# Neighbourhood attention in a two-layer encoder: the two heads of a pair taken together, with the products' order across the halves of the TensorE array changed

## The chip, the cores and the metric

One core of one Trainium2 chip runs the whole program. The metric is device time in microseconds (us) of one execution; three executions of the kernel before gave a median of 902.64 us (899.07 to 903.24).

## The reference, cut to what matters

The program is a two-layer encoder trunk on 256 tokens of 1024 features, in float32. Layer 0 computes from one normed input `h` two things side by side, a state-space scan and a neighbourhood attention with 16 heads of 64 features; both go through one output projection, and a channel mixer follows. Layer 1 is an mLSTM with its own channel mixer. What is changed lies in the attention alone:

```python
q, k, v = jnp.split(qkv.astype(jnp.float32), 3, axis=-1)     # on a grid of 4 rows x 64 columns
...
s = jnp.einsum('bwhd,biwjhd->bhwij', q_r, k_win) + bias.transpose(0, 2, 1, 3)[None]
p = jax.nn.softmax(s.reshape(Bsz, NA_HEADS, GRID_W, kh * NA_KW), axis=-1).reshape(s.shape)
return jnp.einsum('bhwij,biwjhd->bwhd', p, v_win)
```

Each query sees all 4 rows and a window of 16 columns.

## The kernel before

**The weight stream.** Every weight matrix comes in slabs of 128x2048 (1 MB each). A slab is loaded by SyncE (L169) into one of three `raw` buffers. Each of its halves is split into two exact parts, `wh` by ScalarE (L193) and `wl` by VectorE (L194), and three products stand for one exact one: high by high, high by low, low by high (L215 to L217 where weights are the stationary operand, L226 where tokens are). `run` (L145) goes through the list of slabs, and after each half `adv` (L97) advances two queues of side work, `qa` (the scan) and `qb` (the attention), by as many steps as `PLAN0` (L40) gives for that half. A step is what stands between two `yield`s. The instructions are then ordered once, at build time, by a scheduler with a cost model: on each engine an instruction of the earliest place in the program that is ready by the model goes first. On the chip each engine runs this order.

**The attention.** The q and k projections (`na_qk_unit`, L827) leave for each pair of heads a tile `qk`, in which head `i` of the pair holds partitions `64*i` to `64*i+63`. After each k half, `na_side` (L845) of one pair is put on `qb`; there are 8 pairs. A tile of 128 queries is half of the columns of all grid rows (index `f`), and sees 40 columns of each of the 4 rows, 160 keys. In order of its steps, `na_side` does for each head of a pair: two score products (L853, 64 partitions to 128 columns of the stationary operand, 160 moving columns each) into one PSUM bank, the load of the bias table (L857, SyncE), and two fused add-and-minimum operations (L862, VectorE); then two exponentials (L869, ScalarE), the reciprocal (L871) and two scalings (L873, ScalarE) into a padded tile `np`; then four transposes (L878) and a copy to `nap` (L881, ScalarE). After both heads come four value products (L888, 128 partitions to 64 columns, 256 moving columns): both key halves `kk` of head 0, then both of head 1. Head `i` fills output partitions `64*i` to `64*i+63` of one bank, and one copy (L894) takes it to `nay`. These are 7 steps a pair. A float32 product stands in the trace as two weight loads and two matmuls, so there are 4 records of L853 for a head, and 8 of L888 for a pair.

```python
for f in range(2):
    nc.tensor.matmul(out=ps[:, f * 160:(f + 1) * 160], lhsT=qk[rows, 0, f * P:(f + 1) * P], ...)
...
for i in range(2):
    for kk in range(NT):
        nc.tensor.matmul(out=ps[i * 64:(i + 1) * 64, :256], ...)
```

**Banks and buffers.** `bank()` (L79) gives PSUM banks by turns from two pools of two, `sd` and `yp`; scan and attention share them. The projections use four other banks (`acc`). The tiles `rpb` (bias), `nas`, `namx`, `nap` have two buffers each. The scan's products with 48 partitions (L800, L805) build a 128x512 bank that ScalarE takes the exponential of (L808).

Of the kernel before, what the change touches and what calls it, by code (L numbers as in the profile page):

```python
# [10 lines left out]
F32 = mybir.dt.float32  # L11
# [3 lines left out]
ALU = mybir.AluOpType  # L15
# [3 lines left out]
P = 128  # L19
D = 1024  # L20
KT = D // P
NT = 2
# [3 lines left out]
LOW = 1.0e-17  # L26
# [11 lines left out]
SUB_LEAD = 250  # L38
# a slab, steps of the side work (scan, attention) after each half of it, slabs of the modulation after it
PLAN0 = (("v0", 0, 8, 1), ("v1", 0, 5, 0), ("v2", 0, 6, 0), ("q0", 1, 8, 0), ("k0", 4, 3, 0), ("v3", 4, 5, 0),  # L40
# [11 lines left out]
class Trunk:  # L52
# [24 lines left out]

# [1 line left out]
    def bank(self):  # L79
# [32 lines left out]

# [1 line left out]
    # A slab is one transfer; it is split into its two exact parts in `nh` pieces of `hw` columns.  # L114
    def slab(self, ap, nh=2, hw=1024, bufs=None, ada=None, tag=None):
# [93 lines left out]

# [1 line left out]
    def mm_ws(self, out, wh, wl, xh, xl, nk=KT):  # L211
# [16 lines left out]

# [1 line left out]
    def setup(self):  # L230
# [74 lines left out]

    # rows over the partitions, in two exact parts, times a column of ones on both: a broadcast
    def row_parts(self, hi_lo, rows, src):
# [3 lines left out]

# [1 line left out]
    def add_ada(self, layer, j, where):  # L313
# [56 lines left out]

# [1 line left out]
    def squares(self, views):  # L372
# [14 lines left out]

    # the end of a sub-layer for one tile of tokens, and the start of the next
    def sub_end(self, t, banks, out=None):
# [46 lines left out]

    # log(1 + e) for 0 <= e <= 1
    def log1p(self, e, shape):
# [14 lines left out]

# [1 line left out]
    def start(self):  # L455
        nc, io = self.nc, self.io
# [3 lines left out]
        def begin():  # L460
# [16 lines left out]
            self.cbk = [self.abank() for _ in range(4)] + [self.yp.tile([P, 512], F32, name="yp") for _ in range(2)]  # L477
            # zeros, and often enough to have the tensor engine at its full clock when the data arrives
            for i in range(WARM):
# [9 lines left out]

        # the columns of shift and scale for `nb` blocks of features, in slabs of K-tiles  # L490
        def block(kt0, nb, on_pe):
# [61 lines left out]

        # the half that holds B and C goes first
        convs = ([], [])
# [78 lines left out]

    # 32 columns of a projection, to tokens on the rows
    def small_unit(self, name, side):
# [15 lines left out]

# [1 line left out]
    def conv_side(self, pair):  # L654
# [31 lines left out]
    def dt_side(self, ps):  # L686
        nc = self.nc
# [8 lines left out]
        nc.vector.scalar_tensor_tensor(out=self.dt, in0=v, scalar=0.0, in1=l, op0=ALU.max, op1=ALU.add)  # L696
        # where dt is below LOW, ln(dt) = v: what lies below ln(LOW) is added to ln(max(dt, LOW))
        low = self.tmp.tile([P, NT, 32], F32, name="l1p_z", bufs=1)
# [4 lines left out]
        yield  # L703
        # running sums of dt*a inside each chunk: cs (dir, chunk, head), and what is left to its end
        ps = self.bank()
# [13 lines left out]
        self.wst = (dec[:, 4, :], dec[:, 5, :])  # L719
        # ln(dt), with a Newton step, less the running sums  # L720
        v = self.tmp.tile([P, NT, 32], F32, name="dtv", bufs=1)
# [27 lines left out]
    def ssd_side(self):  # L749
# [12 lines left out]
        yield  # L762
        # states carried from one chunk to the other, and their part of y
        for g in range(2):
# [8 lines left out]
            for d in range(2):  # L773
# [14 lines left out]
                yield  # L788
        # inside the chunks, two heads at a time: M[s, t] = (C_t.B_s) * sum over directions of decay * dt_s
        for hp in range(8):  # L790
# [33 lines left out]

# [1 line left out]
    # A tile of queries is half of the columns of all grid rows; it sees 40 columns of each row.  # L826
    def na_qk_unit(self, j, which):  # L827
# [15 lines left out]
        return fn  # L843

    def na_side(self, pair, qk):  # L845
        nc = self.nc
        pts = []
        for i in range(2):
            head = 2 * pair + i
            rows = slice(i * 64, (i + 1) * 64)  # L850
            ps = self.bank()
            for f in range(2):
                nc.tensor.matmul(out=ps[:, f * 160:(f + 1) * 160], lhsT=qk[rows, 0, f * P:(f + 1) * P],  # L853
                                 rhs=qk[rows, 1, :].rearrange("p (r w) -> p r w", w=64)[:, :, f * 24:f * 24 + 40],
                                 start=True, stop=True)
            bias = self.tmp.tile([P, 320], F32, name="rpb")
            nc.sync.dma_start(out=bias, in_=self.io["rpb"][head])  # L857
            s = self.tmp.tile([P, 320], F32, name="nas")
            mx = self.tmp.tile([P, 2], F32, name="namx")
            for f in range(2):  # L860
                fs = slice(f * 160, (f + 1) * 160)
                nc.vector.tensor_tensor_reduce(out=s[:, fs], in0=ps[:, fs], in1=bias[:, fs], op0=ALU.add,  # L862
                                               op1=ALU.min, scale=-1.0, scalar=3.0e38, accum_out=mx[:, f:f + 1])
            yield
            pad = self.npad[i]
            nsum = self.tmp.tile([P, 2], F32, name="nasum")
            win = [pad[:, f].rearrange("p (r w) -> p r w", w=64)[:, :, f * 24:f * 24 + 40] for f in range(2)]
            for f in range(2):
                nc.scalar.activation(out=win[f], in_=s[:, f * 160:(f + 1) * 160].rearrange("p (r w) -> p r w", w=40),  # L869
                                     func=AF.Exp, scale=-1.0, bias=mx[:, f:f + 1], accum_out=nsum[:, f:f + 1])  # L870
            nc.vector.reciprocal(out=nsum, in_=nsum)  # L871
            for f in range(2):
                nc.scalar.activation(out=win[f], in_=win[f], func=AF.Copy, scale=nsum[:, f:f + 1])  # L873
            yield
            ps = self.bank()
            for kk in range(NT):
                for f in range(2):
                    nc.tensor.transpose(out=ps[:, (kk * 2 + f) * P:(kk * 2 + f + 1) * P],  # L878
                                        in_=pad[:, f, kk * P:(kk + 1) * P], identity=self.ident)
            pt = self.tmp.tile([P, 512], F32, name="nap")  # L880
            nc.scalar.copy(out=pt, in_=ps)  # L881
            pts.append(pt)
            yield
        ps = self.bank()
        for i in range(2):
            head = 2 * pair + i
            for kk in range(NT):
                nc.tensor.matmul(out=ps[i * 64:(i + 1) * 64, :256], lhsT=self.v[:, kk, head * 64:(head + 1) * 64],  # L888
                                 rhs=pts[i][:, kk * 256:(kk + 1) * 256], start=(kk == 0), stop=(kk == 1))
# [7 lines left out]

# [1 line left out]
    def rows_mm(self, ps, t, i, wh, wl):  # L899
# [15 lines left out]

    # first columns after a boundary: one tile of tokens after the other
    def rows_head(self, aps, bufs, evac, late):
        nc = self.nc

        def fn(parts):  # L920
            pss = []
            for t in range(NT):
                ps = self.abank()
                ts = slice(t * P, (t + 1) * P)
                # of each half of the features first what needs only their first parts
                for q in range(2):
# [63 lines left out]

    # pairs of feature tiles in two parts, made one ahead of their use
    def pairs_of(self, n, make):
# [97 lines left out]

# [1 line left out]
    def mlp(self, layer, ada_js, head_bufs, out=None):  # L1092
# [49 lines left out]

# [1 line left out]
    def gates_side(self, ps):  # L1144
# [50 lines left out]
        yield  # L1195
        # the floor of the denominator, with tokens on the rows
        self.thr = self.big.tile([P, 2, NT, 8], F32, name="dec")
# [10 lines left out]

    # columns of the score tile of a direction: (dir, key tile) -> (first column, first query, queries)
    SPAN = {(0, 0): (0, 0, 256), (0, 1): (256, 128, 128), (1, 0): (0, 0, 128), (1, 1): (128, 0, 256)}  # L1210
# [31 lines left out]
    def ml_head(self, h, eh, el):  # L1242
# [34 lines left out]
        nc.gpsimd.tensor_tensor(out=ss, in0=ss, in1=self.nhalf, op=ALU.pow)  # L1277
        # half of the norm here, the other half of sigmoid = (1 + tanh) / 2 where the gate arrives
        for t in range(NT):
# [4 lines left out]

    # scores of two heads run ahead of the values
    def ml_side(self):
# [106 lines left out]

# [1 line left out]
def _ws(w):  # L1395
# [105 lines left out]
```

## Time and profile before

| what | value |
|---|---|
| median of three runs | 902.64 us (899.07 to 903.24) |
| profiled execution, first to last instruction (span) | 901.6 us |
| TensorE (PE) busy | 875.1 us, 97% |
| VectorE (DVE) busy | 676.5 us, 75% |
| ScalarE (ACT) busy | 499.0 us, 55% |
| mean granted TensorE clock | 0.994 |
| attention's first score product to its last value product | 99.0 to 242.7 us |

Of the profiled execution only the span is told; it lies 1.04 us below the median of the runs. PE is the matmul, PEld the weight load of the same engine, which overlaps it. Times in rows are microseconds unless marked ns. A busy PE is not PE at its peak: the end of a matmul is modelled, so how densely matmuls follow each other is read from their starts, or from the length of a piece of the chain.

### The profile page before, as it was taken

What the parts mean: (1) busy time and instruction counts of PE and PEld (TensorE: products, weight loads), DVE (VectorE), ACT (ScalarE), POOL (GpSimd) and SP (SyncE); (2) the same over time, 40 slices, a digit from 0 to 9 for tenths busy, and PEclk for the clock granted to TensorE, in tenths of its full rate; (3) what the DMA queues carried; (4) which work ended last, traced back from release to release, by engine and by line L of the source; (5) the groups of instructions that cost most, each with busy time, mean ns of one, the idle gap of its engine ahead of it and who ended that gap; (6) DMA issues with size and microseconds to landing.
All of it is one profiled execution on the core that took longest, in us unless ns stands there. A gap on an engine that the chain in (4) does not pass through costs nothing.

```text
span 901.6 us, 13452 instructions
## 1 busy us (share of the span) xinstructions
PE 875.1 (97%) x5176; PEld 750.6 (83%) x5176; DVE 676.5 (75%) x1098; ACT 499.0 (55%) x870; POOL 45.2 (5%) x68
## 2 busy tenths in 40 slices
PE   7999999999999999999998999999999899999997
PEld 6998887777787898989986998888877699999895
DVE  5869898766688777877777957996978865665754
ACT  3466885656756445445454465777556454444452
POOL 3000000000001000000001000211100100000000
PEclk8999999999999999999999999999999999999999
DMA  9866456524574567777762665645487365665651
GB/s 338 327 223 252 152 189 216 203 96 156 218 276 164 190 237 282 291 281 256 276 265 95 235 233 188 214 186 178 148 293 265 120 235 189 234 233 188 227 187 47
DMA packets 32773, 193.44 MB, mean 215 GB/s; under 512 B 4923, under 2 KB 6971, under 8 KB 11333
## 3 DMA queue, kind: packets, MB, share of 16 engines
q1 hardware_dynamic: 31536, 188.35, 57.4%
q10 hardware_dynamic: 1172, 4.24, 1.3%
q8 instruction: 40, 0.66, 0.3%
q14 instruction: 25, 0.20, 0.1%
HBM read 191.52 MB, written 1.05 MB: 214 GB/s over the span
## 4 chain that ended last, share of the span: by engine, by line
PE 79%; DVE 9%; DMA 6%; ACT 3%; issue 1%; POOL 1%; SPq 0%; POOLq 0%; DVEq 0%; ACTq 0%
PE acc L226 32%; PE acc L215 4%; PE acc L217 3%; PE acc L216 3%; PE yp L217 3%; PE sd L217 3%; PE yp L216 3%; PE yp L215 3%; PE sd L216 3%; PE sd L215 3%; DVE wl L194 3%; PE acc L930 2%; DMA raw<-in_ml_w_out 2%; DMA raw<-in_mlp_w 2%; ACT wh L193 1%
## 5 line engine op out<-in xcount | busy, mean ns | idle before, releaser
L194 DVE TENSOR_TENSOR wl<-raw,wh 128x1024 fp32r<-128x1024 f32 (+1 forms) x234 | 278.5, 1195 | 124.5 <-ACT wh L193 123.8
L193 ACT CAST wh<-raw 128x1024 fp32r<-128x1024 f32 (+1 forms) x234 | 239.2, 1027 | 217.0 <-PE acc L226 81.5
L226 PE MATMUL acc<-wh,uh 128*128 128x512 f32 x352 | 112.5, 392 | 0.3 <-ACT uh L433 0.3
L226 PE MATMUL acc<-wh,ul 128*128 128x512 f32 x352 | 111.9, 391 | 0.9 <-DVE ul L434 0.9
L226 PE MATMUL acc<-wl,uh 128*128 128x512 f32 x352 | 112.3, 391 | 0.2 <-DVE wl L194 0.2
L330 DVE SCALAR_TENSOR_TENSOR ada<-raw,cond,ada 128x1024 f32<-128x1024 f32 x80 | 102.3, 1278 | 3.7 <-DMA raw<-in_ada_w 2.1
L215 PE MATMUL acc<-hh,wh 128*128 128x256 f32 x272 | 79.0, 291 | 1.1 <-ACT xt L1349 0.9
L226 PEld LDWEIGHTS acc<-wh,ul 128*128 128x128 f32 x352 | 65.9, 188 | 15.1 <-DVE ul L434 1.3
L226 PEld LDWEIGHTS acc<-wl,uh 128*128 128x128 f32 x352 | 65.9, 188 | 14.9 <-DVE wl L194 0.6
L216 PE MATMUL acc<-hl,wh 128*128 128x256 f32 x272 | 77.8, 286 | 0.0
L217 PE MATMUL acc<-hh,wl 128*128 128x256 f32 x272 | 77.6, 289 | 0.0
L226 PEld LDWEIGHTS acc<-wh,uh 128*128 128x128 f32 x352 | 63.8, 188 | 12.2 <-ACT uh L433 0.5
L226 PE MATMUL acc<-wh,hh 128*128 128x512 f32 x176 | 70.0, 399 | 0.0
L226 PE MATMUL acc<-wh,hl 128*128 128x512 f32 x176 | 69.6, 396 | 0.0
L226 PE MATMUL acc<-wl,hh 128*128 128x512 f32 x176 | 69.5, 395 | 0.0
L217 PE MATMUL yp<-hh,wl 128*128 128x256 f32 x224 | 63.4, 283 | 0.0
L216 PE MATMUL yp<-hl,wh 128*128 128x256 f32 x224 | 63.4, 283 | 0.0
L217 PE MATMUL sd<-hh,wl 128*128 128x256 f32 x224 | 63.3, 283 | 0.0
L215 PE MATMUL yp<-hh,wh 128*128 128x256 f32 x224 | 63.3, 283 | 0.0
L216 PE MATMUL sd<-hl,wh 128*128 128x256 f32 x224 | 63.3, 283 | 0.0
L215 PE MATMUL sd<-hh,wh 128*128 128x256 f32 x224 | 63.3, 282 | 0.0
L215 PEld LDWEIGHTS acc<-hh,wh 128*128 128x128 f32 x272 | 51.9, 191 | 4.7 <-ACT xt L1349 1.6
(436 smaller groups left out, 1769.2 us busy)
## 6 DMA issues: line engine op xcount, KB each, us to landing
raw<-in_mlp_w SPq DMA_DIRECT2D x60, 1024.0 KB, 4.9
raw<-in_ada_w SPq DMA_DIRECT2D x40, 1024.0 KB, 6.5
raw<-in_ab_w_out SPq DMA_DIRECT2D x8, 1024.0 KB
raw<-in_ml_w_v SPq DMA_DIRECT2D x8, 1024.0 KB, 4.8
raw<-in_ml_w_o SPq DMA_DIRECT2D x8, 1024.0 KB, 4.8
raw<-in_ml_w_out SPq DMA_DIRECT2D x8, 1024.0 KB, 7.5
raw<-in_ada_two SPq DMA_DIRECT2D x4, 1024.0 KB
raw<-in_w_v SPq DMA_DIRECT2D x4, 1024.0 KB
```

What stands on the lines that cost most here:

```text
L193: nc.scalar.copy(out=wh[:, cs], in_=src[:, cs])
L194: nc.vector.tensor_tensor(out=wl[:, cs], in0=src[:, cs], in1=wh[:, cs].bitcast(F32), op=ALU.subtract)
L215: mm(out=out, lhsT=a, rhs=xh[:, k, :], start=(k == 0), stop=False)
L216: mm(out=out, lhsT=a, rhs=xl[:, k, :], start=False, stop=False)
L217: mm(out=out, lhsT=b, rhs=xh[:, k, :], start=False, stop=(k == nk - 1))
L226: mm(out=outs[j], lhsT=x, rhs=w[:, n0 + j * 512:n0 + (j + 1) * 512], start=first and i == 0, stop=last and i == 2)
L330: nc.vector.scalar_tensor_tensor(out=acc, in0=raw[:, q * D:(q + 1) * D], scalar=col, in1=acc, op0=ALU.mult, op1=ALU.add)
L930: nc.tensor.matmul(out=ps, lhsT=x[:, kt, ts], rhs=parts[kt // 2][wi][:, (kt % 2) * 512:(kt % 2 + 1) * 512], start=(kt == 0 and x is self.h ...
```

## The change

`na_side` takes both heads of a pair in each step. The four score products come first, each head into its own bank, in the order head 1, head 0, head 1, head 0, and each is tied behind the one before it on TensorE's queue. All four add-and-minimum operations follow. The bias tables are loaded one pair ahead, by a new function. The softmax of head 1 comes before the transposes of head 0. The value products alternate between head 1 and head 0, which is between the halves of the output's partitions. A pair still has 7 steps and takes 5 banks. The other hunks of the diff take out comments.

```diff
+    def na_bias(self, pair):
+        if pair < 8:
+            self.bias[pair] = [self.tmp.tile([P, 320], F32, name="rpb") for _ in range(2)]
+            for i in range(2):
+                self.nc.sync.dma_start(out=self.bias[pair][i], in_=self.io["rpb"][2 * pair + i])
     def na_side(self, pair, qk):
         nc = self.nc
-        pts = []
+        if pair == 0:
+            self.bias = {}
+            self.na_bias(0)
+        sps = [self.bank() for _ in range(2)]
+        with ExitStack() as order:
+            for f in range(2):
+                for i in (1, 0):
+                    rows = slice(i * 64, (i + 1) * 64)
+                    keys = qk[rows, 1, :].rearrange("p (r w) -> p r w", w=64)[:, :, f * 24:f * 24 + 40]
+                    last = nc.tensor.matmul(out=sps[i][:, f * 160:(f + 1) * 160],
+                                            lhsT=qk[rows, 0, f * P:(f + 1) * P], rhs=keys, start=True, stop=True)
+                    order.enter_context(self.tc.issue_after(last.ins))
+        bias = self.bias.pop(pair)
+        ss, mxs = [], []
         for i in range(2):
-            head = 2 * pair + i
-            rows = slice(i * 64, (i + 1) * 64)
-            ps = self.bank()
-            for f in range(2):
-                nc.tensor.matmul(out=ps[:, f * 160:(f + 1) * 160], lhsT=qk[rows, 0, f * P:(f + 1) * P],
-                                 rhs=qk[rows, 1, :].rearrange("p (r w) -> p r w", w=64)[:, :, f * 24:f * 24 + 40],
-                                 start=True, stop=True)
-            bias = self.tmp.tile([P, 320], F32, name="rpb")
-            nc.sync.dma_start(out=bias, in_=self.io["rpb"][head])
             s = self.tmp.tile([P, 320], F32, name="nas")
             mx = self.tmp.tile([P, 2], F32, name="namx")
             for f in range(2):
                 fs = slice(f * 160, (f + 1) * 160)
-                nc.vector.tensor_tensor_reduce(out=s[:, fs], in0=ps[:, fs], in1=bias[:, fs], op0=ALU.add,
+                nc.vector.tensor_tensor_reduce(out=s[:, fs], in0=sps[i][:, fs], in1=bias[i][:, fs], op0=ALU.add,
                                                op1=ALU.min, scale=-1.0, scalar=3.0e38, accum_out=mx[:, f:f + 1])
-            yield
-            pad = self.npad[i]
+            ss.append(s)
+            mxs.append(mx)
+        self.na_bias(pair + 1)
+        yield
+        for i in range(2):
+            s, mx, pad = ss[i], mxs[i], self.npad[i]
...
             nc.vector.reciprocal(out=nsum, in_=nsum)
+            yield
             for f in range(2):
                 nc.scalar.activation(out=win[f], in_=win[f], func=AF.Copy, scale=nsum[:, f:f + 1])
-            yield
+        yield
+        pts = []
+        for i in range(2):
             ps = self.bank()
...
         ps = self.bank()
-        for i in range(2):
-            head = 2 * pair + i
-            for kk in range(NT):
+        for kk in range(NT):
+            for i in (1, 0):
+                head = 2 * pair + i
                 nc.tensor.matmul(out=ps[i * 64:(i + 1) * 64, :256], lhsT=self.v[:, kk, head * 64:(head + 1) * 64],
                                  rhs=pts[i][:, kk * 256:(kk + 1) * 256], start=(kk == 0), stop=(kk == 1))
```

## Rows read from the trace of the kernel before

**Rows 1.** The page: busy time, share of the span and instructions of two engines.
```profile
PE 875.1 (97%) x5176; PEld 750.6 (83%) x5176; DVE 676.5 (75%) x1098; ACT 499.0 (55%) x870; POOL 45.2 (5%) x68
```

**Rows 2.** Busy time in stretches of the attention; columns in the first line.
```profile
core 0: us, PE busy (x) PEld busy (x) DVE busy (x) ACT busy (x) POOL busy (x), PEclk, DMA share, GB/s
98.00:125.00 27.00, 27.00 (x185) 23.19 (x185) 23.49 (x52) 21.45 (x53) 0.00 (x0) 1.00 0.49 174
125.00:155.00 30.00, 30.00 (x163) 21.94 (x161) 25.77 (x41) 22.23 (x51) 0.95 (x1) 1.00 0.55 189
...
215.00:245.00 30.00, 30.00 (x152) 21.05 (x152) 19.08 (x40) 22.13 (x58) 1.12 (x2) 1.00 0.53 192
sum 147.00, PE 147.00 PEld 112.26 DVE 109.24 ACT 100.83 POOL 3.02; mean PE 29.40 PEld 22.45 DVE 21.85 ACT 20.17 POOL 0.60
```

**Rows 3.** The chain, 98 to 245 us: shares by line, pieces (start, us, what).
```profile
by line: PE acc L226 24.9%; PE acc L216 9.1%; PE acc L215 9.1%; PE acc L217 9.0%; PE yp L888 5.5%; PE sd L888 5.4%; PE sd L853 3.9%; PE yp L853 3.8%; PE sd L878 3.2%; PE yp L800 2.6%; PE yp L878 2.6%; PE sd L819 2.5%; PE sd L783 2.5%; PE yp
...
103.97 0.74 PE sd L853 x4
112.89 0.58 PE sd L888 x2
113.83 1.01 PE sd L888 x6
121.00 0.47 PE yp L853 x2
...
131.96 1.01 PE sd L888 x4
132.97 1.36 PE acc L226 x5
...
162.44 1.16 PE acc L226 x5
167.75 1.75 PE yp L888 x8
169.50 0.74 PE yp L853 x4
```

**Rows 4.** The timeline, 173.2 to 174.6 us: start, us, engine, instruction.
```profile
173.27 0.38 PE L800 MATMUL sd<-csr,pickr 48*128 48x256 f32 x1
173.28 0.18 PEld L853 LDWEIGHTS yp<-qk 64*128 64x128 f32 x1
173.29 0.40 PE L853 MATMUL yp<-qk 64*128 64x160 f32 x1
...
173.53 0.30 PE L853 MATMUL yp<-qk 64*128 64x160 f32 x1
...
173.66 0.30 PE L853 MATMUL yp<-qk 64*128 64x160 f32 x1
...
173.80 0.30 PE L853 MATMUL yp<-qk 64*128 64x160 f32 x1
```

**Rows 5.** Who waited for whom, 98 to 245 us: total, times, longest.
```profile
PEld sd L888 <- ACT nap L881: 1.1, 2, 0.8
...
PEld sd L878 <- ACT np L873: 0.7, 2, 0.4
...
PEld yp L853 <- DVE namx L862: 0.4, 1, 0.4
```

**Rows 6.** Groups of instructions on ACT, 98 to 245 us: busy, mean ns, idle.
```profile
L193 ACT CAST wh<-raw 128x1024 fp32r<-128x1024 f32 x26 | 26.9, 1047 | 9.2 <-PE acc L216 6.5 <-PE acc L226 2.4
...
L881 ACT COPY nap<-sd 128x512 f32<-128x512 f32 x9 | 5.3, 586 | 3.9 <-PE sd L878 3.9
```

**Rows 7.** SyncE's queue, 98 to 245 us: who waited for whom.
```profile
SPq L857 <- DVE namx L862: 41.7, 11, 6.5
```

More of the change, by code (lines that the diff above doesn't have):

```diff
@@ L878, in na_side @@
                     nc.tensor.transpose(out=ps[:, (kk * 2 + f) * P:(kk * 2 + f + 1) * P],
-                                        in_=pad[:, f, kk * P:(kk + 1) * P], identity=self.ident)
+                                        in_=self.npad[i][:, f, kk * P:(kk + 1) * P], identity=self.ident)
             pt = self.tmp.tile([P, 512], F32, name="nap")
```

## The prediction

> **What bounds the kernel now.** I read the busy times first, to see which engine could hold the end: TensorE is busy for 97% of the span, VectorE for 75%, ScalarE for about half [rows 1]. A share of the whole says nothing of one stage, so I then read the stretch that holds the attention, 98 to 245 us: TensorE is busy in all of its 147 us, VectorE in 109, ScalarE in 101, the granted clock is 1.00 (the upper level, 2.4 GHz) and the DMA engines are about half busy [rows 2]. VectorE is nearest to a bound of its own between 98 and 155 us, with 49.3 of 57 us, 86%. The chain of waits comes third: from 98 to 245 us nearly every piece is TensorE's, and the attention's small products stand on it with their whole length [rows 3]. So time taken out of these products is taken out of the end, as long as nobody else becomes late, and the stages behind simply start earlier.
>
> **What the small products cost.** By the shares of the chain the scores (L853) take 3.9 + 3.8 = 7.7% of 147 us, 11.3 us; the values (L888) 5.5 + 5.4 = 10.9%, 16.0 us [rows 3]. The chain lists the scores in 16 pieces and the values in 19. A full score piece of one head, 4 records, is 0.74 us and a piece of 2 records 0.47, so a further record costs about 0.135 us and some 0.20 us of a piece is paid for coming in, however short it is. For values, 4 records are 1.01 us and 2 records 0.58: 0.215 us a record, 0.15 for coming in. Going back to full-array products also costs: five L226 records right behind a value piece are 1.36 us, five behind other work 1.16, so 0.20 us for each return [rows 3]. Six of the 35 pieces stand directly behind another one, and one behind a scan product that also uses only part of the rows; some 28 returns are left.
>
> **The change, part by part.**
>
> *Scores, both heads in one run.* The two heads use opposite halves of the array's rows and write different banks. The question is whether their matmuls then run side by side. The trace of before has one place where this happened by chance: at 173.27 us a scan product on 48 rows and a score product of head 1 start 0.02 us apart, and the four score records keep their own pace (173.29, 173.53, 173.66, 173.80) although scan products run between them [rows 4]. So I take it that head 0's four records hide wholly under head 1's, and a pair's scores cost one piece of 0.74 us: 8 x 0.74 = 5.9 instead of 11.3. **Gain 5.4 us.** Bounds: with no overlap a pair costs 0.74 + 4 x 0.135 = 1.28, in all 10.2, a gain of 1.1; no row suggests more than 5.4.
>
> *Values, alternating.* They overlap by columns, and this too is in the trace: a piece of six records takes 1.01 us, just as one of four does, so two of the six cost nothing [rows 3]. In that piece products of both heads stood side by side, because head 0's first product had gone ahead at 112.89. With head 1, head 0, head 1, head 0 every record has a partner, so 8 records take the time of 4: 8 x 1.01 = 8.1 instead of 16.0. **Gain 7.9 us.** There is a second reason in it: before, head 0's values could start before head 1's transposes were done, which tore them into pieces of two; now the first product needs head 1's probabilities, the last to be ready, and all four follow. Without overlap a pair costs the 1.75 us of the piece of eight [rows 3], in all 14.0, a gain of 2.0.
>
> *Fewer returns.* 16 runs instead of 35 pieces; with one or two of them joined about 15 returns instead of 28: 13 x 0.20. **Gain 2.6 us.** Together 5.4 + 7.9 + 2.6 = 15.9 us.
>
> *Here a rule of the skill speaks against me.* The trace lets a record of the second head pass one of the first, or six records could not fit into four records' time. The Trainium skill ("TensorE: Matmul & The Clock Gate", Part 3) says that matmuls are a strict FIFO in start and end, with no reordering. As one product is two records on the same half, by that rule only every second record would find a partner at once; the piece of six speaks against it. It is a rival below.
>
> *What comes in the way.* The two score banks are taken at once, one of each pool, and both are held until four add-and-minimum operations in a row are done; the scan then has two banks instead of three for a moment. Waits of TensorE on such work are in the trace, but small: 1.1 us in two cases for the copy to `nap`, 0.7 for the scaled probabilities, 0.4 for the reductions [rows 5]. Since the order of the instructions was made by a model before the run, and TensorE now gets through a pair's products about 2 us sooner, it will arrive early more often. The price has no row of its own. At best the 2.2 us of these waits go (a gain); at worst all values of a pair stand behind a cast of 1.05 us and the copy of 0.59 us on ScalarE [rows 6], 1.63 us a pair, 13.1 us in all. I take 0.4 us a pair, nearest to the waits that the trace has: **loss 3.2 us.**
>
> *What costs nothing.* The bias tables: 16 loads as before, on SyncE's queue, now behind both heads' reductions of the pair before. Their waits of before (41.7 us in 11 cases, the longest 6.5) reached no other engine [rows 7], because three slabs of weights are buffered; with 26 casts of half a slab in 147 us [rows 6] a slab lasts some 11 us. If that cover were gone, a wait of 6.5 us would reach TensorE through a late slab. The split of the softmax into other steps moves ScalarE and VectorE work by a step and adds none; it is hidden under projections, with ScalarE at 101 of 147 us. What is late next is VectorE between 98 and 155 us: if a third of the saving falls there, 49.3 us of work stand in 52, so the saving fits but with little room.
>
> **The sum.** 15.9 - 3.2 = 12.7 us off the profiled span of 901.6 gives 888.9; the median of the runs lies 1.04 us above that span, so 889.9, rounded to **890 us**.
>
> **The rivals.**
>
> 1. *FIFO.* If a head's second record can't be passed, a score run costs one slot of 0.135 us more and a value run one of 0.215: 8 x 0.35 = 2.8 us, 892.8 us. For it: only one clean case of passing. Against: that case. This is what the rule named above would give. Chance 0.10.
>
> 2. *Torn runs.* Scan or projection products that become ready in the model may be put between the four products. Before, one head's scores were torn, at 121.00 [rows 3]. A tear of a score run costs 0.20 + 0.20 us, of a value run 0.15 + 0.20; if every run is torn once, 8 x 0.75 = 6.0 us, 896 us. For it: many values were torn before. Against: the scores are now tied behind each other, and the four values wait for the same last copy. Chance 0.12.
>
> 3. *No overlap at all:* the change doesn't do what it says. Gain 1.1 + 2.0 + 2.6 = 5.7, less the waits of 3.2: 900.1 us. Against it stand both rows of overlap; for it, that these were chance meetings, one of them with a scan product of another type. Chance 0.06.
>
> 4. *A dear wait.* The upper bound of the waits, 1.63 us a pair, leaves 2.8 us of the gain: 899.8 us. Chance 0.06.
>
> 5. *Slower: the values wait for the copy of head 1.* Before, head 0's values could fill the time in which ScalarE copies head 1's probabilities to `nap`; now nothing of the values can. If ScalarE has two casts in front of that copy, it comes 2 x 1.05 + 0.59 = 2.68 us late [rows 6], for each of 8 pairs instead of 0.4: 18.2 us, 908 us. It decides from about 2.0 us a pair on (no gain at all), 2.5 for slower by 0.5%. Against it: the copy itself waited for TensorE before, 3.9 us of idle time on ScalarE in one of its two groups [rows 6], not the other way round, and the projections can be put in between. Chance 0.06.
>
> **How the numbers follow.** The forecast (everything overlaps, small waits) has the chance 0.60 that is left. A measurement of this kernel can tell some 0.5% from no change, 4.5 us: faster means below 898.1. That holds for the forecast, the FIFO and the torn runs: 0.60 + 0.10 + 0.12 = 0.82. No overlap and the dear wait are within 0.5%: 0.12. Slower is 0.06. The range goes from all gains with the old waits gone (902.6 - 15.9 - 2.2 = 884.5) up to no overlap, 900.2; outside are the slower case and what I have missed on both sides.
>
> **What would show it.** In the profile after, the chain should list 8 score pieces of about 0.74 us with 8 records and 8 value pieces of about 1.01 with 8; the timeline should show starts of `sd` and `yp` records of the new score line within 0.02 us of each other. Pieces of 1.28 and 1.75 would mean no overlap; 0.9 and 1.2 the FIFO; pieces of 2 or 4 records torn runs. For the waits: the row of TensorE's weight load of the values waiting for `nap` would grow from 1.1 us to some 3 (forecast) or 20 (slower). The prediction is wrong if the stretch from the first score to the last value shrinks by less than 8 us, or if it shrinks as said and the end doesn't, which would mean that a later stage was held by something other than TensorE.

## The result, and the profile after

Changed kernel: **890.32 us**, the median of 4 runs (889.11 to 893.19), beside 900.86 us for the kernel before in the same comparison. The ratio is **0.9902 [0.9878, 0.9925]**, which is 8.8 us off (6.8 to 11.0). The forecast was 890.0, a gain of 12.7 us. The time fell almost on it, the gain did not, so the agreement in time is largely luck: the forecast counted from the first three runs of the kernel before (902.64), which were high; in the comparisons below, with 11 to 23 runs each, its median is 897.9 to 898.8. The two medians above differ by 10.5 us; what is told as the gain here and below is that of the ratio, which comes with an interval.

The page, busy time of the engines, which answers to [rows 1]:

```profile
PE 863.6 (97%) x5176; PEld 745.4 (84%) x5176; DVE 676.5 (76%) x1098; ACT 498.5 (56%) x870; POOL 45.9 (5%) x68
```

The number of records is the same on every engine. TensorE is busy 11.5 us less. The same stretches as in [rows 2], columns as there:

```profile
98.00:125.00 27.00, 24.18 (x174) 20.30 (x173) 22.45 (x45) 20.00 (x49) 0.00 (x0) 1.00 0.48 168
125.00:155.00 30.00, 28.80 (x159) 20.96 (x158) 26.03 (x48) 22.08 (x54) 0.95 (x1) 1.00 0.52 187
...
sum 147.00, PE 142.20 PEld 111.92 DVE 114.24 ACT 103.79 POOL 3.02; mean PE 28.44 PEld 22.38 DVE 22.85 ACT 20.76 POOL 0.60
```

Here is the first thing to see. Before, TensorE was busy in every one of these 147 us; now it sits idle for 4.8 of them, and 4.0 of those lie between 98 and 155 us. VectorE and ScalarE each do more of their work inside the stretch (+5.0 and +3.0 us), because the work behind it has moved up. The granted clock is 1.00 in both, so the clock explains nothing in this stretch.

The products themselves, from the timeline of TensorE (start, us, engine, instruction), the first pair's scores:

```profile
98.45 0.40 PE L864 MATMUL yp<-qk 64*128 64x160 f32 x1
98.45 0.40 PE L864 MATMUL sd<-qk 64*128 64x160 f32 x1
98.69 0.30 PE L864 MATMUL yp<-qk 64*128 64x160 f32 x1
98.69 0.30 PE L864 MATMUL sd<-qk 64*128 64x160 f32 x1
...
112.95 0.39 PE L217 MATMUL acc<-hh,wl 128*128 128x256 f32 x1 [1.24 <-DVE wl L194]
...
122.59 0.50 PE L226 MATMUL acc<-wh,hh 128*128 128x512 f32 x1 [1.31 <-ACT wh L193]
...
143.86 0.39 PE L215 MATMUL acc<-hh,wh 128*128 128x256 f32 x1 [1.20 <-ACT wh L193]
...
167.15 1.08 PE L907 MATMUL yp<-nap,v 128*64 128x256 f32 x8
```

Both heads' records start together, and a pair's four starts take the time that one head took. Seven of the eight score runs are whole, 8 records each; so are seven of the eight value runs (the first pair's is torn into 4 and 4). The three lines with a bracket are new waits: none is the attention's, all three are products of a projection that wait for a part of their weights (`wl` from VectorE, `wh` from ScalarE).

The chain of waits, 98 to 245 us, answers to [rows 3] (start, us, what):

```profile
113.57 1.15 DVE wl L194
114.77 6.70 DMA raw<-in_w_z
121.49 1.04 ACT wh L193
...
125.04 4.75 DMA raw<-in_ada_w
...
134.35 1.20 DVE ada L330
135.57 7.17 DMA raw<-in_w_k
142.76 1.05 ACT wh L193
...
167.21 1.01 PE yp L907 x8
...
169.96 0.33 PE sd L864
170.29 0.13 PE sd L864
170.43 0.13 PE sd L864
170.57 0.13 PE sd L864
```

In the table before, nearly every piece of this chain was TensorE's. Now its first 45 us hold VectorE's splits and three slab loads of 4.75 to 7.17 us, with ScalarE's casts behind two of them and VectorE's multiply-adds (L330) behind the modulation slab: the chain goes through the supply of weights. The score run at 169.96 is 0.33 + 3 x 0.13 = 0.72 us for both heads, the value run 1.01.

**The account.** I add the distances between the starts of TensorE's records, from the first score product to the transposes (L422) that follow layer 0's first output projection:

| us | before | after | difference |
|---|---|---|---|
| whole stretch | 187.2 | 179.1 | -8.1 |
| score records | 11.74 | 6.12 | -5.6 |
| value records | 16.02 | 8.26 | -7.8 |
| entering and leaving them (over the usual spacing of the neighbours) | 5.53 | 2.84 | -2.7 |
| idle before a record that had to wait | 0.9 | 6.3 | +5.4 |
| other spacing, all else | 153.0 | 155.5 | +2.6 |

Which spacing is usual is an estimate, so the rows of entering and of all else hang together: their sum is 158.5 before and 158.3 after. Without that split the account reads: 13.4 us less for scores and values, 5.4 more of idle time, the rest even.

The profiled span fell by more, 901.6 to 889.7, 11.9 us: 8.1 in this stretch, 0.6 ahead of it and 3.2 behind it. What lies behind is not put down to the change: the kernel before waited 2.45 us at 476 us and 0.57 at 467.8, in layer 1, where the profiles of its two variants below (slabs later, parts earlier) show one wait of 0.83, and the kernel after one of 0.84. The whole part behind the stretch is 615.7 us in the profile of before and 612.2 in either variant.

The clock takes a little of the gain there. In layer 1 the profile of the kernel after has a stretch of 3.2 us at a granted clock of 0.50, the lower level (1.2 GHz), where the profile of before has 1.00 (columns as above):

```profile
476.20:479.40 3.20, 3.20 (x9) 2.50 (x9) 2.39 (x6) 0.59 (x1) 0.00 (x0) 0.50 0.49 141
```

Behind the account's stretch the kernel after takes 612.5 us, and its repeat below, which has such a piece at 284.4 us, 613.1. Four variants (scores alone, scores in turn, bias tables, parts earlier), whose clock is 1.00 from 45 to 880 us, take 611.6 to 611.8. By these rows one such piece costs 0.7 to 1.5 us. Why the clock fell there is not shown.

### The profile page after: what moved, and what is told of

Read it like the earlier page. It is cut to its first block, busy times and chain, and to the rows that moved or that the text cites. A ratio compares the mean times of both kernels' runs of the same rounds, so it can differ in the third digit from the quotient of the medians.

```text
span 889.7 us, 13454 instructions
## 1 busy us (share of the span) xinstructions
PE 863.6 (97%) x5176; PEld 745.4 (84%) x5176; DVE 676.5 (76%) x1098; ACT 498.5 (56%) x870; POOL 45.9 (5%) x68
## 4 chain that ended last, share of the span: by engine, by line
PE 85%; DVE 7%; DMA 3%; ACT 2%; issue 1%; POOL 1%; SPq 0%; POOLq 0%; DVEq 0%; ACTq 0%
PE acc L226 40%; PE acc L215 3%; PE yp L217 3%; PE yp L216 3%; PE sd L217 3%; PE yp L215 3%; PE sd L215 3%; PE sd L216 3%; PE acc L217 3%; PE acc L216 3%; PE acc L949 2%; DMA raw<-in_ada_w 1%; DVE wl L194 1%; PE yp L1279 1%; PE sd L1279 1%
## 5 line engine op out<-in xcount | busy, mean ns | idle before, releaser
L330 DVE SCALAR_TENSOR_TENSOR ada<-raw,cond,ada 128x1024 f32<-128x1024 f32 x80 | 102.3, 1279 | 4.3 <-DMA raw<-in_ada_w 3.8
```

The lines of the kernel that those rows point to most:

```text
L330: nc.vector.scalar_tensor_tensor(out=acc, in0=raw[:, q * D:(q + 1) * D], scalar=col, in1=acc, op0=ALU.mult, op1=ALU.add)
```

## The experiments

Twelve runs, one of them the kernel after once more. The first question is whether the halves overlap and by what rule; the second, where a third of the forecast gain (12.7 us, 8.8 measured) went.

**Scores alone.** The kernel after, with the values of head 0 ahead of those of head 1 as before.

```diff
-        for kk in range(NT):
-            for i in (1, 0):
-                head = 2 * pair + i
+        for i in range(2):
+            head = 2 * pair + i
+            for kk in range(NT):
```

> The new scores and softmax order kept, the value products back in the old order (head 0's two, then head 1's two). Theory A (the gain is the array time of both kinds of run: scores 5.6 us, values 7.8 us by the starts in the two profiles, less waits of the full array's products for late weight parts): most of the values' 7.8 us is lost, the value runs are torn into pieces of 0.58 and 1.01 us again, the time stands 3 to 7 us below the kernel before. Rival B (what helps is only that runs are joined; who alternates doesn't matter): as fast as the changed kernel, 8 to 11 us below the kernel before.

Measured: 896.14 beside 898.52 us, 0.9978 [0.9951, 1.0006], 2.0 us with an uncertainty of 2.5, less than was expected. The chain of this kernel, pieces of the values:

```profile
130.01 1.01 PE sd L907 x4
...
163.66 1.63 PE yp L907 x8
...
217.50 1.83 PE sd L907 x8
```

The values are torn again (14 pieces instead of 9), and eight in a row take 1.63 to 1.83 us. The timeline of the last one says why its two heads don't overlap:

```profile
217.43 1.90 PE L907 MATMUL sd<-nap,v 128*64 128x256 f32 x8
217.59 0.60 ACT L900 COPY nap<-yp 128x512 f32<-128x512 f32 x1
...
218.25 0.62 PEld L907 LDWEIGHTS sd<-nap,v 128*64 128x64 f32 x4 [0.20 <-ACT nap L900]
```

Head 0's four records start while ScalarE still copies head 1's probabilities; that copy ends at 218.19, and head 1's first record follows at 218.25, when head 0's last one has started. So products in a row are not enough, they must be ready together. The stretch of the account falls only from 187.2 to 183.6.

**Values alone.** The kernel before, with the four value products alternating.

```diff
-        for i in range(2):
-            head = 2 * pair + i
-            for kk in range(NT):
+        for kk in range(NT):
+            for i in (1, 0):
+                head = 2 * pair + i
```

> The kernel before with only the order of the four value products changed (head 1, head 0, head 1, head 0). Theory A: eight value runs of 1.01 us with 8 records each, 16.0 us on the array become 8.1; with few new waits the time falls by 5 to 8 us. Rival B (the scores' new order is what gives the gain, values are hidden anyway): within 2 us of the kernel before.

Measured: 893.07 beside 898.52 us, 0.9939 [0.9920, 0.9958], a gain of 5.5 us, the larger part of the whole. Its chain:

```profile
134.71 1.01 PE sd L888 x8
```

Eight records in the time of four, with nothing else in the program changed: the value records fall from 16.0 to 8.3 us, and the stretch to 180.3. Most of that arrives at the end, and TensorE idles only 0.6 us between the first score and the last value.

**Values in turn.** The kernel after, with both products of head 1 ahead of both of head 0; nothing else in the program changes, and VectorE and ScalarE run the kernel after's order, instruction for instruction.

```diff
-        for kk in range(NT):
-            for i in (1, 0):
-                head = 2 * pair + i
+        for i in (1, 0):
+            head = 2 * pair + i
+            for kk in range(NT):
```

> The changed kernel, with head 1's two value products ahead of head 0's two; TensorE's order is else the same. Theory A1 (TensorE starts a later record on a free half however far back it stands): runs stay at 8 records in 1.01 us, the time is that of the changed kernel. Theory A2 (a record can pass only its nearest neighbours): only the middle records overlap, a run takes 6 slots, 1.44 us, 3.4 us slower than the changed kernel. Strict order of issue: 7 to 8 slots, 1.7 us a run, 5 to 6 us slower.

Measured: 890.61 beside 898.52 us, 0.9911 [0.9882, 0.9940]: the same as the kernel after. The timeline:

```profile
166.25 1.09 PE L907 MATMUL yp<-nap,v 128*64 128x256 f32 x8
```

The run is as short as with alternation (1.02 us to the next start, beside 1.01). The partners' starts are now 13 ns apart, where they were 6 to 7.

**Scores in turn.** The same question on the rows; here too VectorE's and ScalarE's order is the kernel after's.

```diff
-            for f in range(2):
-                for i in (1, 0):
+            for i in (1, 0):
+                for f in range(2):
```

> The changed kernel, with head 1's two score products ahead of head 0's two; TensorE's order is else the same. Theory A1 (any later record may start on a free half): a run stays at 0.74 us. Theory A2 (only near neighbours pass): 6 slots, 1.01 us, 2.2 us slower over 8 runs. Strict order: 1.15 to 1.28 us a run, 3 to 4 us slower.

Measured: 892.08 us (886.15 to 892.75) beside 898.52, 0.9915 [0.9884, 0.9946]. The timeline, where four records of head 1 now stand ahead of the first of head 0 on the queue:

```profile
98.81 0.40 PE L864 MATMUL yp<-qk 64*128 64x160 f32 x1
98.83 0.40 PE L864 MATMUL sd<-qk 64*128 64x160 f32 x1
99.06 0.30 PE L864 MATMUL yp<-qk 64*128 64x160 f32 x1
99.07 0.30 PE L864 MATMUL sd<-qk 64*128 64x160 f32 x1
```

Head 0's first record starts 13 ns behind head 1's first, and head 1's second comes 0.23 us later. So a record whose half is free starts ahead of earlier ones whose half is taken. This settles the rule: alternation is not what brings the gain. It is enough that the two heads' products stand next to each other and are both ready, which the values of the first experiment were not.

**The bias tables at each pair's own start**, the prefetch of the change undone.

```diff
-        if pair == 0:
-            self.bias = {}
-            self.na_bias(0)
+        self.bias = {}
+        self.na_bias(pair)
...
-        self.na_bias(pair + 1)
```

> The changed kernel, with each pair's bias tables loaded at the pair's own start instead of one pair ahead. Theory: SyncE may issue them as soon as the buffers are free in either case, so within 1 us of the changed kernel. Rival F (the early load is what keeps the reductions on time): VectorE waits for the tables, some 2 us a pair on the first pairs, 3 us or more slower.

Measured: 890.14 beside 898.50 us, 0.9905 [0.9873, 0.9938]. The prefetch brings nothing that can be measured, and costs nothing.

**The modulation slabs later.** For the missing gain the suspicion was the supply of weights between 98 and 155 us. In this stretch the plan puts two modulation slabs behind `k1`, whose work is VectorE's (L330). Here they go behind `k2` and `z1`.

```diff
-         ("q1", 5, 7, 0), ("k1", 6, 8, 2), ("z0", 5, 3, 0), ("q2", 0, 6, 2), ("k2", 5, 0, 0), ("z1", 6, 0, 0),
+         ("q1", 5, 7, 0), ("k1", 6, 8, 0), ("z0", 5, 3, 0), ("q2", 0, 6, 2), ("k2", 5, 0, 1), ("z1", 6, 0, 1),
```

> The changed kernel; in the written order of the slabs the two modulation slabs that stood behind k1 come one behind k2 and one behind z1. TensorE's sums are the same. Theory C (the part of the gain that is missing goes to late weight parts between 105 and 145 us: VectorE's queue is full there, and the load of a weight slab waits for a buffer that VectorE frees late): the waits of 1.24, 1.31 and 1.20 us at 111.7, 121.3 and 142.7 us go or shrink, 2.5 to 4.5 us faster than the changed kernel. Rival D (the missing part is lost in the attention's own chain, to two banks held at once and longer softmax steps): no difference over 1 us.

Measured: 892.28 beside 898.50 us, 0.9931 [0.9910, 0.9953]: no better. The early waits do go, from 1.24 us to 0.49 at the first, the two others wholly; the gain is given back 170 us later. Timeline and then chain of this kernel:

```profile
110.66 0.39 PE L217 MATMUL acc<-hh,wl 128*128 128x256 f32 x1 [0.49 <-DVE wl L194]
...
277.98 1.11 PE L422 MATMUL yp<-ident,xn 128*128 128x128 f32 x4 [5.83 <-DVE xn L418]
```

```profile
260.44 7.78 DMA raw<-in_mlp_w1h
...
268.24 0.63 ACT wh L193
...
277.18 0.76 DVE xn L418
```

At the end of the sub-layer TensorE waits 5.83 us for the normed rows; in the kernel after that wait is 0.75. The chain says why: a cast on ScalarE stands in its fixed queue ahead of the sums of squares, and waits for a slab that started its load at 260.44. From 276 to 284 us, in and behind this wait, the granted clock is 0.57 on average.

**The same move in the kernel before.**

> The kernel before with the same move of two modulation slabs. Theory C: TensorE had no such waits there before, so within 1.5 us of the kernel before. Rival E (the move helps either kernel, since VectorE was late in both): 2.5 to 4.5 us faster than the kernel before.

Measured: 901.75 beside 898.50 us, 1.0032 [1.0015, 1.0050], 2.9 us slower, where within 1.5 was expected. So the move is no improvement of its own that the test above would have mixed in. It has a cost of its own, and in the test above such a cost may hide a gain from the waits that went.

**The kernel after, once more**, for a second profile.

> The changed kernel once more, as a measure for the others of this call: 0.988 to 0.993 of the kernel before.

Measured: 890.07 beside 898.50 us, 0.9905 [0.9878, 0.9931]. Waits stand at the same places: 1.23 us at 111 and 0.83 at 120.5, for weight parts as before; the 0.35 at 141.8 is another one, a product of the scan that waits for VectorE. In the account, idle time is 5.0 us instead of 6.3 and all else 155.9 instead of 155.5, the stretch 178.1. The first two waits belong to the kernel, their sizes vary by half a microsecond.

**Weight parts placed earlier.** The scheduler's lead for the splits in layer 0, raised from 125 to 250, so that casts and subtractions go ahead of the scan's work on VectorE.

```diff
-LEADS = (125, 75, 50, 75)
+LEADS = (250, 75, 50, 75)
```

> The changed kernel, with the priority of the weight parts in layer 0 raised (first of LEADS 125 to 250), so that casts and subtractions stand ahead of more scan and modulation work in the queues of ScalarE and VectorE. Theory C (VectorE's order in front of the weight parts costs the waits between 105 and 145 us): the wait of 1.2 us at 111 us, behind eight convolution steps, goes; the two that hang on a late load may shrink; 1 to 3 us faster than the changed kernel. Rival D (lost in the attention's own chain): no difference over 1 us, and longer waits of the attention's products.

Measured: 891.18 beside 897.86 us, 0.9920 [0.9897, 0.9942]; no gain. The wait at 111 is gone; others stand at 118 (0.46), 137 (0.77), 217 and 221 (0.76 each), 243.5 (1.12) and 248 (1.62).

**Both, slabs later and parts earlier.**

> Both: the raised priority and the two modulation slabs behind k2 and z1. Theory C: all three waits go, and the end of layer 0 doesn't get the wait of 5.8 us that the move alone had, since there the sum of squares stands ahead of the late cast in ScalarE's queue as in the changed kernel; 3 to 5 us faster than the changed kernel, near 886 us. Rival: the late loads come back at the end of the layer in any order, no gain.

Measured: 897.12 beside 897.86 us, 0.9980 [0.9960, 0.9999]. The expectation was missed by far: two edits that each remove the waits they aim at lose nearly all of the change's gain together. Its timeline shows one of the new waits:

```profile
223.82 0.50 PE L226 MATMUL acc<-wh,uh 128*128 128x512 f32 x1 [2.47 <-ACT wh L193]
```

A part of this loss is the clock. Two us behind that wait the granted clock falls to 0.50 (226 to 229 us). The 12 runs of this kernel list a mean clock of 0.986 to 0.995, and the time goes with it: 897.55 and 899.50 us at 0.986, 891.61 and 892.02 at 0.995, where the kernel after has 889.21.

**Parts earlier in the kernel before.**

> The kernel before with the raised priority. Theory C: no waits for parts were there to remove, within 1.5 us of the kernel before. Rival (the priority is of use in itself): 2 us or more faster.

Measured: 896.21 beside 897.86 us, 0.9978 [0.9964, 0.9991], 2.0 us faster, where within 1.5 was expected. The same setting that does nothing for the kernel after helps the one before a little.

**Two slabs less.** The last test takes load away rather than moving it: the two modulation slabs behind `k1` are neither loaded nor worked on.

```diff
-        a = self.spread([(0, 2), (0, 3), (0, 4)])
+        a = self.spread([(0, 2), (0, 3), (0, 4)], skip=(1, 2))
...
+        q = deque(v for n, v in enumerate(q) if n not in skip)
...
-         ("q1", 5, 7, 0), ("k1", 6, 8, 2), ("z0", 5, 3, 0), ("q2", 0, 6, 2), ("k2", 5, 0, 0), ("z1", 6, 0, 0),
+         ("q1", 5, 7, 0), ("k1", 6, 8, 0), ("z0", 5, 3, 0), ("q2", 0, 6, 2), ("k2", 5, 0, 0), ("z1", 6, 0, 0),
```

> The changed kernel without the two modulation slabs behind k1: their loads and their four multiply-adds on VectorE (5.1 us) are left out, so the gate of layer 0's first sub-layer lacks a half of its sum. Theory C (the waits between 105 and 145 us come from VectorE's load and from buffers held by those slabs): the waits at 111.7, 121.3 and 142.7 us go, TensorE idles under 1 us between 98 and 240 us, and the last value product stands 3 to 5 us earlier against the first score product than in the changed kernel; the time falls by as much unless the end of the layer takes it back, as it did when the slabs were moved. Rival G (waits of this size turn up anywhere once TensorE's small products are shorter): the idle time between 98 and 240 us stays at 3 to 5 us, at other places.

Measured: 892.25 beside 898.79 us, 0.9928 [0.9903, 0.9953]. The waits at 121 and 142 us are gone, the one at 111 falls to 0.50. But TensorE's timeline has this at another place:

```profile
213.77 0.33 PE L898 MATMUL sd<-ident,np 128*128 128x128 f32 x1 [2.04 <-ACT np L891]
```

Between the first score and the last value TensorE idles 3.5 us, as in the repeat of the kernel after (3.4), where under 1 us was expected, and the last value product stands only 1.7 us earlier against the first score product (0.6 beside the repeat), where 3 to 5 was expected. These two slabs and the buffers that they hold are not what holds the time. But with this edit, and with the moved slabs and the raised lead, VectorE and ScalarE also got another order (in the two kernels with the products in turn they did not), so the runs don't tell the next late engine from a new order.

## Why the prediction was right, and where not

**The scores** (gain 5.4): measured 5.6. Two rows of overlap in the trace of before were enough to price it.

**The values** (7.9): measured 7.8, and 7.7 in the kernel with the values alone. The second reason held too: with head 1 last, seven of eight runs are whole.

**Fewer returns** (2.6): 2.7 by the account's split. Together 16.1 beside 15.9. As nearly the same amount (2.6) comes back in the spacing of all other records, it is not shown that this gain arrived. The Trainium skill says that changing the tiling mode drains TensorE ("TensorEngine Tiling (Array Packing)", Tiling Modes, Key Properties); the trace agrees as far as it shows a price, 5.53 us before and 2.84 after by that split, and shows no drain as such.

**The waits** (loss 3.2): this is the step that failed. The three gains less the fall of the stretch, 16.1 - 8.1, leave 8.0 us lost in this profile: 5.4 in new idle time of TensorE, 2.6 in the spacing of all other records. In the repeat it is 16.1 - 9.1 = 7.0. "I take 0.4 us a pair, nearest to the waits that the trace has" was priced on the wrong rows. Those were the attention's own waits, for `np`, `nap` and `namx` [rows 5], and these grew little: over all rows of that view from 3.7 to 4.3 us. Who waited for whom, 98 to 245 us (total, times, longest):

```profile
PEld sd L897 <- ACT np L890: 1.5, 3, 1.1
...
PEld yp L907 <- ACT nap L900: 1.2, 3, 0.4
...
PEld sd L907 <- ACT nap L900: 1.1, 3, 0.4
...
PEld acc L215 <- ACT wh L193: 1.6, 2, 1.4
...
PEld acc L226 <- ACT wh L193: 1.5, 1, 1.5
...
PEld acc L217 <- DVE wl L194: 1.4, 1, 1.4
```

The values' wait for `nap` is 2.3 us in six cases, where some 3 was forecast. The other three rows, 4.5 us, are projections waiting for weights, and nothing of that was in the sum. The text had named the place, "What is late next is VectorE between 98 and 155 us", and judged by the sum that the work "fits but with little room". A busy share of 86% says whether work fits into a stretch; it doesn't say whether a given tile comes in time. And the price was read from rows of the old order, while the scheduler orders the changed kernel anew, on every engine. The wait at 112.95 shows what that does. VectorE's queue, timeline of the kernel before and then of the kernel after:

```profile
108.83 1.65 DVE L669 SCALAR_TENSOR_TENSOR cva<-y,convw,cva 128x256 f32<-128x256 f32 x4
110.40 1.22 DVE L194 TENSOR_TENSOR wl<-raw,wh 128x1024 fp32r<-128x1024 f32 x1
```

```profile
108.50 3.26 DVE L669 SCALAR_TENSOR_TENSOR cva<-y,convw,cva 128x256 f32<-128x256 f32 x8
111.67 1.22 DVE L194 TENSOR_TENSOR wl<-raw,wh 128x1024 fp32r<-128x1024 f32 x1
```

The last lines of the two are the same split. Four steps of the convolution stood right ahead of it, now all eight do, 3.26 us, and it comes 1.27 us later. TensorE's order changed too. The first product that needs this split (by the count of records), in the timeline of before, and the first pair's values in the timeline of after:

```profile
115.11 0.28 PE L217 MATMUL acc<-hh,wl 128*128 128x256 f32 x1
```

```profile
113.72 0.65 PE L907 MATMUL sd<-nap,v 128*64 128x256 f32 x4
```

Before, the values (112.89 and 113.83 in [rows 3]) stood ahead of that product and filled the time; now it stands ahead of them, at 112.95, and waits. A quicker TensorE isn't the reason here: shortly before, at 109.39 us, its records stand 0.61 us earlier than in the kernel before, and the first score product did by 0.60 already. The second wait has the same form: that product came at 125.20, behind the second pair's scores (121.00 in [rows 3]), and is now asked for at 121.28, ahead of them. Its slab came hardly later than before: a `raw` buffer came free at 114.7, the load was issued at 114.77 (114.91 before) and took 6.70 us, and the cast began at 121.49 (121.09 before), 1.8 us after ScalarE was free for it. In the third the load was issued at 135.57 (135.85 before) and took 7.17 us, and the cast began at 142.76 (142.19). So the slabs came about when they came before, and the cover named for the loads, three buffered slabs, did not last for an order that asks earlier. The bias tables had no part in it: their own waits on SyncE's queue fell, where [rows 7] had 41.7:

```profile
SPq L849 <- DVE namx L874: 5.1, 6, 1.5
```

**The rivals.** The FIFO (892.8) is refuted by the kernels with the products in turn. The Trainium skill says of matmuls "strict FIFO, no reordering" ("TensorE: Matmul & The Clock Gate", Part 3). By that rule, in the kernel with the scores in turn, head 0 would have started only behind head 1's last record, 0.51 us after its first; the rows show 13 ns, and the measurement decides. Torn runs came once in each kind, 0.75 us by the price in the text. No overlap is refuted by the timelines after. In the slower rival the values wait for the last copy: that was 2.3 us, in place of some 20. The dear wait had the right kind (a loss of several us) at the wrong place.

**The marker** "the stretch from the first score to the last value shrinks by less than 8 us" was badly chosen: that stretch shrank by 1.7 us only (143.6 to 141.9), so by this sign as it was written the prediction failed. The scheduler also moved other work into the stretch: it holds 864 records of TensorE where it held 834. Up to the end of the sub-layer the same kernel gains 8.1.

**What is shown and what is open.** Shown: the overlap and its size, that the order within a run is free as long as both heads are ready, that the bias prefetch is worth nothing here, that the missing gain is mostly new idle time of TensorE, whose largest pieces are the three late weight parts (1.24 + 1.31 + 1.20 = 3.75 us), and that in front of the first two of them the build put TensorE's and VectorE's work into another order. Shown as well that taking away the named causes (slabs later, slabs left out, parts earlier) did not bring the gain back. Open is why: each of these edits also made a new order, and the times that the scheduler's model reckoned with are not on record. Whether a plan of slabs exists that keeps the whole 16 us is open; no version tried beat the kernel after by more than the noise. A fourth `raw` buffer would test the supply directly; it wasn't tried.

## What to carry to other kernels

Look in the trace of before for small products on opposite halves of the array's rows, or of its output columns, that meet by chance, and price the change by them. Here the second product cost next to nothing (8 score records 0.745 us, 4 alone 0.738) when it stood next to its partner and was ready at the same time, and its full time when it was not. When such a change shortens the engine that bounds the kernel, price the other engines' queues and the buffers by what must be ready when, not by busy shares. Where a scheduler orders the instructions at build time, a change to one part orders the others anew: compare the orders of both kernels around each new wait. An edit that removes one named wait proves the wait, not the gain; look for the same microseconds further on, and at the clock.

## What the runs showed of the hardware that was not expected

A matmul on a free half passed up to three earlier records of the other half, by rows and by columns. With the products alternating, partners started 6 to 7 ns apart, with the products in turn 13 ns, and the total was the same.
